# Tying the filler matmuls of layer 0's attention to the score product three key tiles back

## The chip, the cores and the metric

The kernel runs on one core of one Trainium2 chip. The metric is the device time of one execution in microseconds (us); lower is better. The core has five engines that work in parallel, each strictly through its own list of instructions: PE (TensorE, matrix products; its weight loads are shown as PEld), DVE (VectorE), ACT (ScalarE), POOL (GpSimd) and SP (SyncE, which issues the DMAs here). An instruction that needs another engine's result waits for a semaphore, and everything behind it on the same engine waits with it.

## What is computed

Two layers of a transformer over 1024 latent tokens and a prefix of 256 context tokens, width 1024, in 32-bit floats. Layer 0, which the change concerns, is attention in two head groups, each head with a SiLU gate:

```
aq, ak, av, ag, bq, bk, bv, bg = split_cols(h @ w_in, EVEN_WIDTHS)
oa = gqa_attend(qa_blk, ka, va)            # A: 8 heads, 2 KV heads, over all 1280 keys
ob = gqa_attend(qb, kk, vv, bias, sink)    # B: 8 heads, 2 KV heads, band of +-128 plus context, with a sink
y  = concat([oa * silu(ag), ob * silu(bg)]) @ w_out
x  = x + g * y
```

Here `h` is the RMS-normed input, scaled and shifted by vectors from `silu(c) @ mod_w + mod_b` ("modulation"). Layer 1 is a convolution module beside a neighbourhood attention, then a final norm.

## The kernel before

**Products in three parts.** To keep 32-bit precision each operand is split into a high and a low part (`split`, L298 a cast on ACT, L301 a subtraction on POOL or DVE), and `mm3` (L320 to L322) makes each product of high x high, high x low and low x high.

**Units and key tiles.** Layer 0's attention runs as four units, each one KV head with its four query heads, in the order `ORDER = (2, 3, 0, 1)`: units 2 and 3 are the window heads (B), units 0 and 1 the global heads (A). A unit has ten groups, one for each block of 128 queries; a group goes over 2 to 5 key tiles (B) or 2 or 10 (A). So there are 42 key tiles in a window unit and 84 in a global one, 252 in all.

**One group** (`attn_prep`, `attn_gen`). Ahead of a group its Q is loaded from DRAM (`QH`, `QL`), and the maximum of the scores is found: products `mx` (L578 for the context, L590 or L598 for the rest) into two PSUM banks, each reduced by DVE (L580, L591, L599), then `nmt` (L379 to L385), a transposition `trn` (L389), and L390, which writes the maximum into `QL`. For each key tile PE makes the score `st` in two halves, L467 with `QH` and L471 with `QL` (which holds the low part of Q and the maximum), into one of two PSUM banks; ACT takes the exponential (L479) and casts it (L298), POOL or DVE makes the low part (L301), and three tiles later (`LOOK0 = 3`) PE adds the three products with V into `ov` (L411 to L413), which has one bank. At the end of a group DVE divides (L421 to L424, L633, L635).

**Fill.** Between the steps of attention the kernel weaves other work, so that PE has something to do while attention waits for the other engines: the projections of the next unit (`proj_qkv`: products `pq`, with their transpositions `trk` in `qk_tail`), gate projections (`proj_gate`: `pg`), the modulation vectors (`mod_half_v`: multiply-adds `macc` of the DMAed `mw` on DVE, L221, and small sums `trm` on PE, L227), and in the last unit the output projection of the units already done (`out0`: `po`). `proj_qkv` writes K, Q and V to DRAM (L843, L844, L822) and they are loaded again (L553, L554, L565) when their unit is near. The buffers of K and V also serve for `mw` before the first unit.

**What sets the order.** `weave(main, nmain, fill, nfill, ...)` takes `nmain` steps of the attention generator (two steps for each key tile) and spreads `nfill` steps of fill over them. For the first three units it is called for a gate block, then for the next unit's projections (`NFILL` steps), then for the last `NLAST` steps, 28 in window units and 48 in global ones, with no fill. The written order is not the order on the chip: a scheduler goes over the program with a timeline of its own and picks, on each engine, the instruction of highest priority that is ready there. Fill is traced with a priority 80 places lower (`later(FL[0])`), so it comes in where the scheduler finds PE with nothing else, and it may then come in far ahead of its written place. `tc.issue_after(ins)` binds the instructions traced inside it, as far as they are on the engine of `ins`, to stand behind `ins` in that engine's list. It costs no semaphore and no instruction. `weave` has a parameter `lag` for this: with `lag = n` every fill step stands behind the score product L467 that is n back in `sts`, the list of all score products traced so far. Layer 1 uses it with 0, 0, 6 and 12; layer 0 leaves it at 0:

```python
                    if lag and len(sts) >= lag:
                        cx.enter_context(tc.issue_after(sts[-lag].ins))
                    next(fill, None)
```

Of the kernel before, what the change touches and what calls it, by code (L numbers as in the profile page):

```python
# [68 lines left out]
GB = 2  # L69
NFILL = (43, 43, 40)  # L70
GL = 12
HV = (('gggvvvvg',) * 3, ('gggvvvvg', 'vvvgvvvg', 'gggvvvvg'))
O1 = (6, 65, 41, 14)
TICK0, TICK1 = (1, 3)
# [15 lines left out]
def tile_kernel(ctx: ExitStack, tc: tile.TileContext, a, out):  # L90
# [406 lines left out]
    def weave(main, nmain, fill, nfill, last=True, all_fill=True, lag=0):  # L497

        done = 0
        for k in range(nmain):  # L500
            next(main, None)
            while done * nmain < (k + 1) * nfill:
                with ExitStack() as cx:
                    cx.enter_context(later(FL[layer[0]]))
# [3 lines that stand above are left out]
                done += 1  # L508
        if all_fill:
            for _ in fill:  # L510
                pass
        if last:
            for _ in main:
                pass
# [136 lines left out]
    NSTEP = (168, 84)  # L651


    with ExitStack() as p0x:
# [114 lines left out]
        def proj_gate(u, ms):  # L769

            if u not in gw:
                gw[u] = load_g0(u) if u == ORDER[0] else load_w0("ev_g", u, 256)
            wh, wl = gw[u]
            for m, c in ms:
                t0, n = CHUNKS[c]
                pp = bank("pp", nm("pg"))
                for dk in range(DK):
                    ms_ = slice(m * P, (m + 1) * P)
                    mm3(pp[:, :n], wh[dk][:, ms_], wl[dk][:, ms_], Hs(h, 0, t0, n, dk), Hs(h, 1, t0, n, dk),
                        dk == 0, dk == DK - 1)  # L780
                    if dk % 3 == 1:
                        tick()
                        yield
                sg = ap.tile([P, 640], F32, tag="rt2", name=nm("sg"), bufs=2)
                silu2(pp[:, :n], sg[:, :n])
                mark[0] = SY.dma_start(Gs[u][:, m, t0 : t0 + n], sg[:, :n])
                for _ in range(2):
                    if tails:
                        qk_tail(*tails.pop(0))
# [96 lines left out]
        for k in range(4):  # L886
            u = ORDER[k]
            n = NSTEP[u // 2] + (12 if k == 0 else 0)
            if k < 3:
                n0 = N0[1 + u // 2] if k else N0[0]  # L890
                n1 = n - n0 - NLAST[u // 2]
                weave(main, n0, proj_gate(u, gblocks(k)[1]), 9, False)
                weave(main, n1, fill0(k + 1), NFILL[k], False)
                weave(main, NLAST[u // 2], iter(()), 0, False)
            else:
                weave(main, GL, proj_gate(u, gblocks(k)[1]), 18 - 3 * GB, False)
        run(mods)


# [76 lines left out]
    with tc.tile_pool(name="o0", bufs=1, reuse_waits="tile", side="right") as op_:  # L976
        U1 = ORDER[-1]
# [88 lines left out]
                next(fp[0])  # L1066
                yield

        weave(main, O1[0], load_oh(parts[0]), 6, False)
        weave(main, O1[1], out0_part(parts[0]), 48, False)  # L1070
        weave(main, O1[2], chain(load_oh(parts[1]), out0_part(parts[1])), 30, False)
        ws = [load_w(op_, a["ev_wo"], e2 * 256, 256, 256, WO, lambda dk: "gv"[dk % 2], dks=final, rb=2) for e2 in range(4)]
        fp = [final_proj(c) for c in range(3)]
        nh = [norm_h(0, "st", "tr"), norm_h(1, "pp", "tr"), norm_h(2, "st", "tr")]
        weave(main, NSTEP[U1 // 2] - GL - O1[0] - O1[1] - O1[2], through_attention(), O1[3])
        a0x.close()
        solo[0] = True
        layer[0] = 1
# [564 lines left out]
```

## Time and profile before

| | |
|---|---|
| median of 3 runs | 1567.05 us |
| the three runs | 1563.86, 1573.72, 1567.05 us |
| span of the profiled execution (no other time of it is recorded) | 1569.6 us |
| mean granted TensorE clock | 0.961 |
| busy: PE, DVE, POOL, ACT | 1460.8, 1129.4, 830.0, 762.0 us |
| layer 0's attention, from its first score product to its last product with V | 160.6 to 911.9 us |

The page of the profile gives for each engine the busy time and its share of the span, and the chain of work that ended last, by engine. The windows view gives the same busy times for chosen stretches, with the TensorE clock that was granted in each (1.00 is full) and the share of the DMA engines. The timeline lists one engine's instructions by start time and length; products on PE are pipelined, so the distance of two starts tells the pace, not the length. In brackets stand an idle time before an instruction and what ended it. In names `x<-y,z`, x is written and y, z are read.

### The profile page before, as it was taken

Reading aid. Unit: us, or ns where it says so; the run is one execution under the profiler, and the core shown is the slowest. Engines: PE = TensorE matmul, PEld = TensorE weight load, DVE = VectorE, ACT = ScalarE, POOL = GpSimd, SP = SyncE. Lnnn points to the kernel's source line nnn. Section 1 sums busy time; section 2 is a strip of 40 time slices with the busy share of each in tenths; the row PEclk is TensorE's granted clock in tenths of the full one; section 3 lists DMA queues with packets and bytes.
Section 4 is the critical chain, followed back from the end, with each engine's and each line's share of the span. In section 5 each row is a group of like instructions: output and inputs, shape, how many; then the busy total and the mean of one; then the engine's idle time right before and its main releaser. Section 6 shows DMA issues by size and latency. Waiting matters only on the chain.

```text
span 1569.6 us, 22251 instructions
## 1 busy us (share of the span) xinstructions
PE 1460.8 (93%) x6984; PEld 1178.9 (75%) x6984; DVE 1129.4 (72%) x2172; ACT 762.0 (49%) x1545; POOL 830.0 (53%) x762
## 2 busy tenths in 40 slices
PE   6989999998999999899999889999999999899995
PEld 1878877876888677588887568888887787677784
DVE  4898896797768677455488668999654466776776
ACT  2721354545454754655555746443343445545472
POOL 1561463555465675756545756665443333444575
PEclk9899999999999999999999989999999999799897
DMA  9548245424431225612112022214547888889632
GB/s 337 190 142 260 87 142 167 132 67 125 154 116 47 67 91 167 224 47 61 48 38 85 14 94 61 81 58 148 177 154 224 237 229 242 248 231 251 187 95 108
DMA packets 199438, 221.03 MB, mean 141 GB/s; under 512 B 18956, under 2 KB 155352, under 8 KB 199320
## 3 DMA queue, kind: packets, MB, share of 16 engines
q1 hardware_dynamic: 192656, 208.04, 43.5%
q10 hardware_dynamic: 6664, 11.57, 2.3%
q8 instruction: 55, 0.90, 0.2%
q14 instruction: 63, 0.52, 0.1%
HBM read 159.51 MB, written 60.03 MB: 140 GB/s over the span
## 4 chain that ended last, share of the span: by engine, by line
PE 65%; DVE 14%; DMA 11%; issue 4%; POOL 2%; SPq 2%; ACT 1%; ACTq 0%; DVEq 0%; POOLq 0%
PE p L322 6%; PE p L321 6%; PE p L320 6%; PE ov L411 4%; PE ov L413 4%; PE ov L412 4%; PE po L320 4%; PE po L321 4%; PE po L322 4%; PE st L467 4%; PE st L471 4%; DMA mw<-in_mod_w_dram 3%; DVE macc L221 2%; PE pq L322 2%; PE pq L321 2%
## 5 line engine op out<-in xcount | busy, mean ns | idle before, releaser
L301 POOL TENSOR_TENSOR pl<-pf,ph 128x512 fp32r<-128x512 f32 (+4 forms) x321 | 393.7, 1237 | 320.1 <-ACT ph L298 260.0
L301 POOL TENSOR_TENSOR wl<-wr,wh 128x256 fp32r<-128x256 f32 (+2 forms) x256 | 197.5, 788 | 203.1 <-ACT wh L298 192.4
L479 ACT ACTIVATE pf<-st 128x512 f32<-128x512 f32 x284 | 167.3, 597 | 177.4 <-PE st L471 138.3
L298 ACT CAST ph<-pf 128x512 fp32r<-128x512 f32 (+4 forms) x364 | 210.5, 588 | 28.9 <-PE ov L412 21.5
L298 ACT CAST wh<-wr 128x256 fp32r<-128x256 f32 (+2 forms) x264 | 102.8, 404 | 172.9 <-DMA wr<-in_ev_qkv_dram 40.4
L320 PE MATMUL p<-hh,wh 128*128 128x512 f32 x448 | 177.5, 398 | 2.9 <-DVE spk L301 1.5
L321 PE MATMUL p<-hl,wh 128*128 128x512 f32 x448 | 178.0, 398 | 0.2 <-POOL hl L301 0.2
L322 PE MATMUL p<-hh,wl 128*128 128x512 f32 x448 | 175.9, 400 | 0.1
L467 PE MATMUL st<-QH,KAt 128*128 128x512 f32 (+4 forms) x364 | 145.4, 401 | 11.4 <-ACT pf L479 9.7
L411 PE MATMUL ov<-ph,Vt 128*128 128x512 f32 (+4 forms) x364 | 143.5, 394 | 9.7 <-ACT ph L298 5.0
L413 PE MATMUL ov<-pl,Vt 128*128 128x512 f32 (+4 forms) x364 | 144.1, 396 | 6.8 <-POOL pl L301 3.6
L471 PE MATMUL st<-QL,KBt 68*128 68x512 f32 (+4 forms) x364 | 139.0, 391 | 5.8 <-DVE QL L390 5.7
L412 PE MATMUL ov<-ph,Vt 128*64 128x512 f32 (+4 forms) x364 | 140.5, 386 | 0.0
L1122 DVE SCALAR_TENSOR_TENSOR cps<-U,taps,cps 128x512 f32<-128x512 f32 x184 | 124.3, 748 | 0.0
L591 DVE TENSOR_REDUCE mp<-mx 128x1 f32<-128x512 f32 x128 | 85.7, 682 | 42.5 <-PE mx L590 41.8
L221 DVE SCALAR_TENSOR_TENSOR macc<-mw,csil,macc 128x512 f32<-128x512 f32 x107 | 94.5, 901 | 17.5 <-DMA mw<-in_mod_w_dram 16.7
L320 PEld LDWEIGHTS p<-hh,wh 128*128 128x128 f32 x448 | 84.6, 189 | 23.6 <-DVE spk L301 1.7
L321 PEld LDWEIGHTS p<-hl,wh 128*128 128x128 f32 x448 | 84.5, 189 | 20.4 <-POOL hl L301 0.6
L322 PEld LDWEIGHTS p<-hh,wl 128*128 128x128 f32 x448 | 84.8, 189 | 20.1 <-POOL wl L301 0.6
L467 PEld LDWEIGHTS st<-QH,KAt 128*128 128x128 f32 x364 | 71.2, 196 | 33.4 <-ACT pf L479 17.6
L413 PEld LDWEIGHTS ov<-pl,Vt 128*128 128x128 f32 x364 | 71.1, 195 | 32.5 <-POOL pl L301 7.8
L411 PEld LDWEIGHTS ov<-ph,Vt 128*128 128x128 f32 x364 | 71.3, 196 | 27.3 <-ACT ph L298 8.4
(277 smaller groups left out, 3546.2 us busy)
## 6 DMA issues: line engine op xcount, KB each, us to landing
mw<-in_mod_w_dram SPq DMA_DIRECT2D x34, 512.0 KB, 5.9
Q<-qs SPq DMA_DIRECT2D x40, 256.0 KB, 2.7
QH<-Q SPq DMA_DIRECT2D x80, 128.0 KB, 2.8
wr<-in_od_d_dram SPq DMA_DIRECT2D x64, 128.0 KB, 2.7
mw<-in_mod_w_dram SPq DMA_DIRECT2D x28, 256.0 KB, 3.3
wr<-in_ev_qkv_dram SPq DMA_DIRECT2D x32, 192.0 KB, 3.6
KAt<-KD SPq DMA_DIRECT2D x16, 384.0 KB, 6.2
wr<-in_od_wo_dram SPq DMA_DIRECT2D x48, 128.0 KB, 3.2
```

Source lines behind the costliest of these rows:

```text
L221: VE.scalar_tensor_tensor(t, w, csil[:, dk, q : q + 1], t, op0=ALU.mult, op1=ALU.add)
L298: SC.copy(hi, src)
L301: (GP if leng == "g" else VE).tensor_tensor(lo, src, hi.bitcast(F32), op=ALU.subtract)
L320: PE.matmul(o, lh, rh, start=first, stop=False)
L321: PE.matmul(o, lh, rl, start=False, stop=False)
L322: done[0] = PE.matmul(o, ll, rh, start=False, stop=last)
L411: PE.matmul(o, V[:, 64:192], ph[:, :n], start=(t == 0), stop=False)
L412: PE.matmul(g.ov[0:64, q0 : q0 + n], V[:, 0:64], ph[:, :n], start=False, stop=False)
L413: pvs.append(PE.matmul(o, V[:, 64:192], pl[:, :n], start=False, stop=(last and g.sink is None)))
L467: sts.append(PE.matmul(st[:, :n], KA[:, cs], g.QH[:, q0 : q0 + n], start=True, stop=False))
L471: PE.matmul(st[:, :n], KB[0:68, cs], g.QL[0:68, q0 : q0 + n], start=False, stop=True)
L479: SC.activation(pf[:, :n], st[:, :n], AF.Exp, scale=1.0 if g.bias else SCALE)
```

## The change

All weave calls of layer 0 that have fill get `lag = 3`. So no PE instruction of a fill step may stand ahead of the first half (L467) of the score product that was third from last when the step was traced. While fewer than three score products are traced, there is no bound. Instructions of fill on DVE, ACT, POOL and SP are not bound by it, but they get their results from PE. All priorities, step counts and buffers stay.

```diff
+LAG0 = 3
...
-                weave(main, n0, proj_gate(u, gblocks(k)[1]), 9, False)
-                weave(main, n1, fill0(k + 1), NFILL[k], False)
+                weave(main, n0, proj_gate(u, gblocks(k)[1]), 9, False, True, LAG0)
+                weave(main, n1, fill0(k + 1), NFILL[k], False, True, LAG0)
                 weave(main, NLAST[u // 2], iter(()), 0, False)
             else:
-                weave(main, GL, proj_gate(u, gblocks(k)[1]), 18 - 3 * GB, False)
+                weave(main, GL, proj_gate(u, gblocks(k)[1]), 18 - 3 * GB, False, True, LAG0)
...
-        weave(main, O1[0], load_oh(parts[0]), 6, False)
-        weave(main, O1[1], out0_part(parts[0]), 48, False)
-        weave(main, O1[2], chain(load_oh(parts[1]), out0_part(parts[1])), 30, False)
+        weave(main, O1[0], load_oh(parts[0]), 6, False, True, LAG0)
+        weave(main, O1[1], out0_part(parts[0]), 48, False, True, LAG0)
+        weave(main, O1[2], chain(load_oh(parts[1]), out0_part(parts[1])), 30, False, True, LAG0)
...
-        weave(main, NSTEP[U1 // 2] - GL - O1[0] - O1[1] - O1[2], through_attention(), O1[3])
+        weave(main, NSTEP[U1 // 2] - GL - O1[0] - O1[1] - O1[2], through_attention(), O1[3], True, True, LAG0)
```

The order of the instructions shows what the scheduler makes of it. The line numbers of the changed kernel are one higher. First PE at the start of the attention, where the second halves of the first two scores stand; `pq_` and a number is one block of 24 projection products. Before, five whole blocks and most of a sixth (`pq_2039`) stand ahead of them:

```order
L320 MATMUL pq_2039<-wh_1460,hh_171 128x384
L321 MATMUL pq_2039<-wl_1461,hh_171 128x384
L322 MATMUL pq_2039<-wh_1460,hl_172 128x384
L320 MATMUL pq_2039<-wh_1466,hh_171 128x384
L321 MATMUL pq_2039<-wl_1467,hh_171 128x384
L471 MATMUL st_1527<-QL_1271,KBt_1254 128x512
L471 MATMUL st_1544<-QL_1271,KBt_1254 128x512
L322 MATMUL pq_2039<-wh_1466,hl_172 128x384
```

With the change, at the same two halves, the second block (`pq_1695`) follows them:

```order
L599 MATMUL mx_1484<-KAt_1262,QH_1282 128x384
L599 MATMUL mx_1487<-KAt_1262,QH_1282 128x384
L390 MATMUL trn_1391<-ident,nmt_1375 12x128
L579 MATMUL mx_1622<-KAt_1262,QH_1522 128x256 x2
L579 MATMUL mx_1639<-KAt_1262,QH_1522 128x256 x2
L472 MATMUL st_1527<-QL_1271,KBt_1254 128x512
L472 MATMUL st_1544<-QL_1271,KBt_1254 128x512
L599 MATMUL mx_1643<-KAt_1262,QH_1522 128x384
L599 MATMUL mx_1675<-KAt_1262,QH_1522 128x384
L468 MATMUL st_1585<-QH_1270,KAt_1262 128x512
L472 MATMUL st_1585<-QL_1271,KBt_1254 128x512
L321 MATMUL pq_1695<-wh_1430,hh_169 128x384
```

Only one block is left ahead of these halves; the maximum products of the second and third group have moved up between the first maximum and its score.

The second place is PE near the end of the first unit (key tile 28, `st_2735`), whose maximum comes through `QL_2418`. Before, the next unit's projections stand in the gaps:

```order
L320 MATMUL pq_3280<-wh_3275,hc_168 128x384
L321 MATMUL pq_3339<-wl_3270,hc_168 128x384
L322 MATMUL pq_3339<-wh_3269,hc_168 128x384
L320 MATMUL pq_3339<-wh_3275,hc_168 128x384
L321 MATMUL pq_3280<-wl_3276,hc_168 128x384
L322 MATMUL pq_3280<-wh_3275,hc_168 128x384
L321 MATMUL pq_3339<-wl_3276,hc_168 128x384
L322 MATMUL pq_3339<-wh_3275,hc_168 128x384
L598 MATMUL mx_2878<-KAt_1262,QH_2730 128x256
L471 MATMUL st_2735<-QL_2418,KBt_1254 128x512
```

With the change the same score stands among attention alone:

```order
L414 MATMUL ov_2782<-pl_2704,Vt_1255 128x512
L417 MATMUL ov_2782<-QL_2168,sk 128x512
L599 MATMUL mx_2856<-KAt_1262,QH_2730 128x256
L599 MATMUL mx_2869<-KAt_1262,QH_2730 128x256
L390 MATMUL trn_2688<-ident,nmt_2678 12x128
L599 MATMUL mx_2875<-KAt_1262,QH_2730 128x256
L599 MATMUL mx_2878<-KAt_1262,QH_2730 128x256
L472 MATMUL st_2735<-QL_2418,KBt_1254 128x512
```

The `pq` products have moved behind, into the next unit's written place.

The third place is PE near the end of the last unit (key tile 240, `st_9476`). Before, the output projection is already done there:

```order
L411 MATMUL ov_9389<-ph_9419,Vt_1259 128x512
L412 MATMUL ov_9389<-ph_9419,Vt_1259 64x512
L467 MATMUL st_9476<-QH_8876,KAt_5695 128x512
L471 MATMUL st_9476<-QL_8877,KBt_1258 128x512
L413 MATMUL ov_9389<-pl_9420,Vt_1259 128x512
L411 MATMUL ov_9389<-ph_9444,Vt_1259 128x512
L412 MATMUL ov_9389<-ph_9444,Vt_1259 64x512
```

With the change its blocks `po` stand between the key tiles:

```order
L321 MATMUL po_9368<-hh_7480,wh_9227 128x512
L322 MATMUL po_9368<-hl_7481,wh_9227 128x512
L323 MATMUL po_9368<-hh_7480,wl_9228 128x512
L468 MATMUL st_9476<-QH_8876,KAt_5695 128x512
L472 MATMUL st_9476<-QL_8877,KBt_1258 128x512
L412 MATMUL ov_9389<-ph_9444,Vt_1259 128x512
L413 MATMUL ov_9389<-ph_9444,Vt_1259 64x512
L321 MATMUL po_9402<-hh_7480,wh_9233 128x512
```

So fill has moved from the middle of the unit to its end. From layer 1 on PE's order is the same in both.

## The prediction

> **What bounds the kernel now.** I read the page's busy times first, then the chain of work that ended last, then the windows view over stretches cut at the score products of layer 0, then the waits of PE inside the poor stretches.
>
> ```profile
> PE 1460.8 (93%) x6984; PEld 1178.9 (75%) x6984; DVE 1129.4 (72%) x2172; ACT 762.0 (49%) x1545; POOL 830.0 (53%) x762
> ...
> PE 65%; DVE 14%; DMA 11%; issue 4%; POOL 2%; SPq 2%; ACT 1%; ACTq 0%; DVEq 0%; POOLq 0%
> ```
>
> PE is busy for 93% of the span and makes 65% of the chain. So time moves only if PE idles less, or runs at a lower granted clock for a shorter time. Layer 0's attention has 252 key tiles (window heads 0 to 83, global heads 84 to 251); I count them by their first score product (L467) in the order of PE. The next rows are the windows view, cut where the tiles 0, 6, 12, 24, 48, 54, 60, 72, 90, 114, 120, 126, 144, 156, 228 and 246 start; the first row is the time just before tile 0 and the last the tail. Columns: length, busy time by engine, granted PE clock, DMA.
>
> ```profile
> 152.30:160.60 8.30, 7.88 (x53) 7.66 (x53) 7.05 (x12) 1.26 (x3) 2.18 (x3) 1.00 0.77 234
> 160.60:191.30 30.70, 30.24 (x172) 27.88 (x171) 25.94 (x57) 10.87 (x25) 14.94 (x12) 1.00 0.22 66
> 191.30:206.60 15.30, 12.68 (x51) 8.46 (x51) 14.32 (x29) 7.44 (x18) 7.82 (x7) 0.78 0.20 61
> 206.60:248.50 41.90, 39.56 (x207) 32.23 (x206) 37.08 (x77) 23.10 (x57) 29.16 (x26) 1.00 0.53 162
> 248.50:347.30 98.80, 96.22 (x502) 82.80 (x500) 77.48 (x170) 44.33 (x94) 48.45 (x39) 1.00 0.40 123
> 347.30:359.90 12.60, 10.78 (x51) 7.64 (x51) 10.72 (x27) 7.88 (x19) 6.20 (x5) 1.00 0.19 54
> 359.90:387.10 27.20, 21.36 (x113) 17.84 (x111) 21.58 (x56) 11.98 (x28) 13.70 (x13) 0.99 0.45 139
> 387.10:445.30 58.20, 56.88 (x284) 47.16 (x284) 45.48 (x96) 27.27 (x61) 28.10 (x25) 0.95 0.50 155
> 445.30:503.30 58.00, 58.00 (x300) 51.89 (x299) 42.32 (x80) 28.01 (x54) 33.98 (x28) 1.00 0.23 68
> 503.30:543.30 40.00, 36.72 (x156) 25.08 (x155) 25.48 (x49) 28.00 (x47) 28.69 (x23) 1.00 0.15 42
> 543.30:560.80 17.50, 16.71 (x90) 14.76 (x89) 13.13 (x24) 10.68 (x23) 12.87 (x12) 1.00 0.39 119
> 560.80:576.60 15.80, 12.92 (x48) 9.27 (x47) 10.49 (x20) 8.08 (x17) 11.75 (x11) 0.78 0.20 60
> 576.60:638.90 62.30, 59.94 (x294) 47.32 (x293) 47.24 (x77) 35.75 (x64) 38.76 (x26) 1.00 0.57 177
> 638.90:665.40 26.50, 22.41 (x89) 16.56 (x88) 9.40 (x18) 15.41 (x29) 21.25 (x21) 0.87 0.67 221
> 665.40:852.90 187.50, 187.50 (x892) 151.56 (x892) 117.69 (x211) 99.02 (x181) 106.13 (x91) 1.00 0.18 52
> 852.90:891.50 38.60, 34.77 (x140) 23.84 (x138) 26.68 (x46) 24.21 (x44) 24.02 (x20) 0.91 0.13 45
> 891.50:914.00 22.50, 15.56 (x61) 10.77 (x62) 18.02 (x27) 14.70 (x26) 13.67 (x10) 0.81 0.03 9
> ```
>
> I call "loss" the length less PE's busy time, plus the missing share of the clock times the length. From the second row on: 0.5, 6.0, 2.3, 2.6, 1.8, 6.1, 4.2, 0, 3.3, 0.8, 6.4, 2.4, 7.5, 0, 7.3 us: 51.2 us in 731 us, of which 42.4 after tile 24. This is all that any reordering here can win. It sits where fill is missing. Counting the fill matmuls of each stretch in the order of before, and giving each 0.175 us (384 wide) or 0.23 us (512 wide), from the spacing of rows quoted below, the rows at 191.30, 347.30, 503.30, 560.80, 638.90 and 852.90 hold 0.4, 0.4, 0.3, 0.3, 3.5 and 3.2 us of fill for 72 tiles, and lose 32.3 us. The row at 665.40 holds 90 us of fill for 72 tiles and loses nothing.
>
> Loss per tile from these rows, the prices of everything below:
> - window heads without fill: (6.0 + 1.8) / 12 = 0.65 us, ends 0.30 and 1.0;
> - window heads with fill: 2.6 + 6.1 + 4.2 over the 54 tiles from 24 on that have it (72 to 83 lose nothing): 0.24 us;
> - global heads without fill: (3.3 + 6.4 + 7.5 + 7.3) / 60 = 0.41 us, ends 0.14 (row 503.30) and, over more than one group, 0.63 (row 638.90);
> - global heads with fill: (0.8 + 2.4) / 102 = 0.03 us.
>
> **The change, part by part.** It adds no instruction and no semaphore; only the place of PE rows moves, and what other engines then get later. The fill's own PE work is the same in both. Three terms follow.
>
> *The start, tiles 0 to 24.* These rows of PE's timeline show the first maximum products (L578), the first halves of the first two scores, two neighbours of the 384-wide fill, and the second halves (L471, which need the maximum in QL).
>
> ```profile
> 160.06 0.70 PE L578 MATMUL mx<-KAt,QH 128*128 128x256 f32 x4 [0.42 <-DMA V<-vs]
> 160.59 0.63 PE L467 MATMUL st<-QH,KAt 128*128 128x512 f32 x2
> ...
> 161.58 0.34 PE L321 MATMUL pq<-wl,hh 128*128 128x384 f32 x1
> 161.76 0.34 PE L322 MATMUL pq<-wh,hl 128*128 128x384 f32 x1
> ...
> 182.13 0.62 PE L471 MATMUL st<-QL,KBt 68*128 68x512 f32 x2
> ```
>
> Before, 31 fill matmuls fill the time up to 160.06, and 109 more stand between there and the second half of the score at 182.13, so the chain from maximum to QL costs PE next to nothing. Now 7 of the 31 and all of the 109 stand behind it: 24 are ahead of L471 instead of 140. At 152.30 PE finds only two mod reductions and then waits for KAt, whose load SP issued here:
>
> ```profile
> 157.16 1.28 SPq L553 DMA_DIRECT2D KAt<-K  x3
> ```
>
> That load follows the last reading of its buffer by a mod product on DVE, and in the new DVE order two more mod instructions stand ahead of that one: about 1.2 us later, so the first maximum product starts near 161.3. From there DVE sets the pace: PE may go ahead only as DVE hands back the two mx banks. Between the first maximum and QL the new DVE order has 4 L580, 8 L599 (four of 256, four of 384, each with its readout), 7 mod products and one L390.
>
> ```profile
> L221 DVE SCALAR_TENSOR_TENSOR macc<-mw,csil,macc 128x512 f32<-128x512 f32 x30 | 27.9, 939 | 6.8 <-DMA mw<-in_mod_w_dram 6.4
> L580 DVE TENSOR_REDUCE mp<-mx 128x2 f32<-128x512 f32 x16 | 10.7, 683 | 0.9 <-PE mx L578 0.9
> L599 DVE CUSTOM_DVE_ANT_0 mx<-mx,k_bm 128x384 f32<-128x384 f32 x18 | 10.0, 563 | 2.1 <-PE mx L598 1.9
> L390 DVE TENSOR_TENSOR QL<-trn,k_bd 12x512 fp32r<-12x512 f32 x6 | 4.1, 682 | 0.2
> L599 DVE DVE_READ_ACCUMULATOR2_ANT mp<- 128x1 f32 x22 | 2.8, 126 | 0.1
> L599 DVE CUSTOM_DVE_ANT_0 mx<-mx,k_bm 128x256 f32<-128x256 f32 x4 | 1.7, 420 | 0.0
> ```
>
> 4 x 0.683 + 4 x 0.420 + 4 x 0.563 + 8 x 0.126 + 7 x 0.939 + 0.682 = 14.9 us, on from about 161.7: QL near 176.6, against 182.13. Attention starts 5.5 us earlier, but with 116 x 0.175 = 20.3 us less fill done, so PE is 14.8 us behind. What comes back: at tile 24 both orders have done the same fill (138 to 139 us by the count). Before needed 66.4 us from 182.1 to 248.5, of which 8.8 were loss, so 57.6 of work. Now it is 57.6 + 20.3, less 1.5 for the maximum products already done, = 76.4: tile 24 at 253.0 with no loss at all, at 257.6 with 0.19 us per tile (row 206.60: 2.3 over 12 filled tiles). That is +4.5 to +9.1 us. I take +9.1, since rows with fill in the window heads do lose. It cannot be much under +4.5, PE's own floor. DVE, busy for 14.32 of 15.30 us in row 191.30 and 37.08 of 41.90 in row 206.60, has the same work to do up to tile 24 and is no further behind, so it adds no term of its own.
>
> *The ends of units.* The order now keeps to the written plan, with no fill in the last steps of each unit. Tiles 30 to 36 and 72 to 84, which held 7.5 and 13 us of fill, now hold 0 and 2; tiles 144 to 162 held 12 and hold none; 126 to 144, 162 to 168 and 180 to 192 hold 16 us where 55 stood. At these places the second half of a score waits for QL with only attention in between. Such a wait is in the trace:
>
> ```profile
> 385.88 0.73 PE L471 MATMUL st<-QL,KBt 68*128 68x512 f32 x2 [4.47 <-DVE QL L390]
> ```
>
> Prices: 18 window tiles without fill x 0.65 = 11.7 (ends 5.4 and 18). 18 global tiles without fill x 0.41 = 7.4; 36 with a little fill at half of that, 7.4 (together ends 5 and, with no credit and at 0.63, 34).
>
> *The places that get fill.* Tiles 48 to 54, 90 to 114 with 120 to 126, and 228 to 246, whose rows held 0.3 to 3.2 us, now get 14, 34 and 21 us, mostly 6 to 7 us for six tiles, which is what the row at 665.40 has (90 us for 72). They are priced as filled. The other 42 window tiles from 24 on: 42 x 0.24 = 10.1. The other 108 global tiles: 108 x 0.03 = 3.2. The tail behind tile 246 (row 891.50) has the same order of PE but for one sum of squares, and costs nothing new: the 13 last blocks of out-projection stand between it and the first product that needs its result.
>
> After tile 24: 11.7 + 7.4 + 7.4 + 10.1 + 3.2 = 39.8 against 42.4, so -2.6 us. The sum is +9.1 - 2.6 = +6.5 us on the profiled 1569.6, 1576.1; that execution lies 2.55 us over the median of the three runs, so 1573.5 against 1567.05. SP and POOL: the loads of Q for the next groups now stand ahead of a V write that waits for fill, which only helps; the splits of weights on ACT and POOL are not bound and stay hidden behind PE.
>
> **A rule of the clock.** These rows show PE's products before and after the longest gap between 191.3 and 206.6, 1.44 us: 512-wide products follow each other at 0.43 us after it and at 0.24 again from 202.48 on, and the clock of row 191.30 is 0.78.
>
> ```profile
> 197.78 0.79 PE L467 MATMUL st<-QH,KAt 128*128 128x512 f32 x1 [1.44 <-ACT pf L479]
> 200.50 0.63 PE L412 MATMUL ov<-ph,Vt 128*64 128x512 f32 x1
> 200.93 0.63 PE L413 MATMUL ov<-pl,Vt 128*128 128x512 f32 x1
> 202.48 0.40 PE L411 MATMUL ov<-ph,Vt 128*128 128x512 f32 x1
> 202.72 0.40 PE L412 MATMUL ov<-ph,Vt 128*64 128x512 f32 x1
> ```
>
> [...] I keep the rows' prices; as a rival this lies within 1%, and I give it 0.05.
>
> **Rivals.**
> 1. *Slower: the QL wait of each group.* In the poor stretches nothing covers the chain from maximum to QL, so each group of heads waits there. 18 window tiles are about 4 groups, 54 global ones about 5: 9 waits at the 4.47 us of row 385.88 are 40 us against the 26.5 priced above, so +13.7: 1587. It passes 1% (1582.7) when a wait is over about 4.1 us. For it: row 385.88, and the 6.0 us of row 191.30. Against it: row 503.30 loses 3.3 us over two and a half groups without fill.
> 2. *Faster: even fill is worth more than its price.* If filled window tiles lose nothing, as 445.30 shows, global ones without fill 0.14, and the start +4.5: 11.7 + 2.5 + 2.5 + 3.2 = 19.9, so -22.5 + 4.5 = -18.0: 1549. Against it: rows 359.90 and 387.10 have fill and still lose 10.3 us.
> 3. *No effect: the poor stretches only change places.* The start stays at PE's floor, +4.5, the rest is -2.6: 1569. That the edit does nothing at all is excluded by the order, in which most PE rows of layer 0's attention move.
>
> **How the numbers follow.** A measurement of this kernel can tell about 1%, 15.7 us, from no change: 1551.4 to 1582.7. My forecast, rival 3 and the clock's case lie within it, together 0.60; rival 1 has 0.28, rival 2 has 0.12. The predicted time is the sum, 1573. Ends: all cheap ends together give +4.5 + (5.4 + 5 + 10.1 + 3.2 - 42.4) = -14.2, about 1553; the dear ones +9.1 + (18 + 34 + 10.1 + 3.2 - 42.4) = +32, 1599. With rival 2 a little under the cheap end and rival 1 at 1587, I give 1551 to 1594 for 8 in 10.
>
> **What would show it.** Right: PE idle between 153 and 177 of about 15 us, the first L471 near 177, tile 24 later than 248.5 by 4 to 9 us; windows at tiles 90 to 126 and 228 to 246 with PE full and the clock at 1.00; new losses of about 0.65 us a tile at 30 to 36 and 72 to 84 and 0.4 at 144 to 162. Wrong: no loss at the unit ends (then it is faster), waits of more than 4 us for QL at each group (slower), or a moved loss in layer 1, whose order is the same.

## The result and the profile after

The changed kernel took 1604.74 us (median of 4 runs, 1603.14 to 1609.25), the kernel before 1570.38 us beside it (4 runs, 1563.86 to 1575.45): ratio 1.0247, 95% interval 1.0211 to 1.0283. It is slower by 2.5%. The prediction was 1573 us with a range of 1551 to 1594; the measured time lies above it.

The busy times of the page of the changed kernel (span 1603.9 against 1569.6):

```profile
PE 1476.2 (92%) x6984; PEld 1185.4 (74%) x6984; DVE 1132.6 (71%) x2172; ACT 762.2 (48%) x1545; POOL 831.6 (52%) x762
```

PE is busy 15 us longer for the same 6984 products, and the rest of the 34 us is idle time. The windows view of the changed kernel, cut at tiles 0, 6, 12, 24, 30, 36, 42, 72, 84, 126, 144, 162, 168, 180, 192, 228 and 246, and the row behind tile 246 (columns as in the prediction):

```profile
161.30:192.20 30.90, 26.89 (x116) 22.17 (x116) 20.46 (x55) 10.24 (x25) 10.40 (x9) 0.79 0.16 49
192.20:212.20 20.00, 19.65 (x110) 17.57 (x108) 15.91 (x29) 7.63 (x17) 11.61 (x10) 1.00 0.18 53
212.20:261.00 48.80, 44.91 (x234) 38.18 (x232) 41.15 (x77) 24.53 (x58) 31.73 (x27) 0.97 0.49 148
261.00:291.90 30.90, 24.22 (x112) 17.36 (x110) 22.95 (x67) 10.41 (x25) 5.11 (x4) 0.92 0.50 158
291.90:304.30 12.40, 11.73 (x37) 8.52 (x38) 4.97 (x8) 8.51 (x17) 8.43 (x7) 0.64 0.15 44
304.30:321.60 17.30, 15.47 (x81) 12.53 (x80) 12.39 (x36) 8.60 (x17) 7.00 (x6) 1.00 0.22 69
321.60:448.00 126.40, 120.86 (x619) 102.48 (x617) 99.13 (x216) 57.65 (x131) 72.31 (x57) 1.00 0.43 133
448.00:475.40 27.40, 25.23 (x108) 18.81 (x109) 22.24 (x47) 16.95 (x32) 15.52 (x12) 0.88 0.24 73
475.40:591.70 116.30, 115.28 (x572) 97.74 (x571) 81.57 (x144) 61.26 (x115) 70.51 (x56) 1.00 0.23 70
591.70:642.20 50.50, 43.63 (x203) 31.93 (x202) 39.73 (x71) 28.60 (x57) 34.60 (x31) 0.93 0.44 133
642.20:672.20 30.00, 27.63 (x110) 17.71 (x109) 17.32 (x32) 22.19 (x38) 22.23 (x18) 1.00 0.13 38
672.20:687.20 15.00, 13.84 (x57) 9.68 (x56) 7.92 (x17) 8.32 (x15) 9.17 (x8) 1.00 0.03 10
687.20:723.40 36.20, 36.20 (x161) 28.70 (x161) 13.53 (x25) 19.33 (x31) 21.19 (x14) 1.00 0.39 125
723.40:751.40 28.00, 22.53 (x82) 16.10 (x81) 11.46 (x20) 18.08 (x33) 22.84 (x17) 0.82 0.76 261
751.40:876.80 125.40, 125.17 (x605) 101.41 (x605) 76.67 (x138) 53.27 (x104) 60.42 (x57) 1.00 0.16 49
876.80:920.70 43.90, 43.82 (x204) 34.90 (x202) 32.67 (x53) 24.99 (x47) 24.75 (x20) 1.00 0.10 37
...
920.70:1603.90 683.20, 627.84 (x2950) 508.01 (x2950) 483.97 (x946) 323.73 (x672) 344.94 (x362) 0.96 0.55 164
```

Read by the prediction's measure (length less PE busy, plus the missing clock), the losses down the rows are 10.5, 0.4, 5.4, 9.2, 5.1, 1.8, 5.5, 5.5, 1.0, 10.4, 2.4, 1.2, 0, 10.5, 0.2, 0.1: 69.2 us where there were 51.2. The rows that were poor before, 84 to 126 and 228 to 246, are full now. The start loses 10.5 us in tiles 0 to 6, where the kernel before lost 6.0 one row later. Behind it three rows stand out: 24 to 30 (9.2), 126 to 144 (10.4) and 180 to 192 (10.5). The same three stretches before, from its windows view (the second stands in the prediction):

```profile
248.50:297.00 48.50, 47.02 (x253) 40.52 (x252) 33.37 (x79) 19.45 (x42) 17.09 (x16) 1.00 0.62 189
...
731.20:762.70 31.50, 31.50 (x155) 25.70 (x154) 15.78 (x33) 16.50 (x31) 17.19 (x15) 1.00 0.12 34
```

They lost 1.5, 2.4 and 0, with 34, 31 and 17 us of fill, counted and priced as in the prediction; now they have 8, 9 and 4.

Where the 34.3 us lie: tile 24 comes 12.5 us later (261.0 against 248.5), the way from tile 24 to tile 246 is 16.7 us longer (659.7 against 643.0, the same fill in both), and the part behind tile 246 is 5.1 us longer (683.2 against 678.1).

PE's waits from tile 24 into the tail, changed kernel (engine, line, tile, releaser: us in total, times, longest):

```profile
PE mx L591 <- DVE mp L592: 6.2, 9, 1.8
PE ov L412 <- ACT ph L299: 4.3, 3, 2.6
PE ov L414 <- DVE pl L302: 3.5, 2, 2.4
PE st L468 <- ACT pf L480: 3.1, 6, 1.2
...
PE trn L390 <- DVE modT L229: 2.6, 1, 2.6
...
PE bc L264 <- DVE nr L244: 2.3, 1, 2.3
```

No wait is long. The largest sum is that of the maximum products for a bank that DVE has not read yet. The second half of a score waits for QL less than before; the same view from tile 24 to tile 246, kernel before and changed kernel:

```profile
PE st L471 <- DVE QL L390: 5.7, 2, 4.5
...
PE st L472 <- DVE QL L391: 1.2, 3, 0.7
```

### The profile page after: what moved, and what is told of

It reads as the page before. It is cut to its first block, busy times and chain, and to the rows that moved or that the text cites. A ratio compares the mean times of both kernels' runs of the same rounds, so it can differ in the third digit from the quotient of the medians.

```text
span 1603.9 us, 22241 instructions
## 1 busy us (share of the span) xinstructions
PE 1476.2 (92%) x6984; PEld 1185.4 (74%) x6984; DVE 1132.6 (71%) x2172; ACT 762.2 (48%) x1545; POOL 831.6 (52%) x762
## 5 line engine op out<-in xcount | busy, mean ns | idle before, releaser
L412 PE MATMUL ov<-ph,Vt 128*128 128x512 f32 (+4 forms) x364 | 143.4, 394 | 10.4 <-ACT ph L299 7.1
L472 PE MATMUL st<-QL,KBt 68*128 68x512 f32 (+4 forms) x364 | 141.4, 396 | 3.2 <-DVE QL L391 3.2
```

The lines of the kernel that those rows point to most:

```text
L412: PE.matmul(o, V[:, 64:192], ph[:, :n], start=(t == 0), stop=False)
L472: PE.matmul(st[:, :n], KB[0:68, cs], g.QL[0:68, q0 : q0 + n], start=False, stop=True)
```

## The experiments

Two theories stood after the result. "Places": each stretch pays by itself for the fill that it lacks. "Late start": the late first maximum leaves other work behind, and the later stalls follow from it. The times of the kernel before are those taken beside each group of runs: 1564.85, 1565.48, 1567.16, 1567.11 and 1567.48 us. The experiments carry the numbering of the kernel before, so their lines are one less than those of the changed kernel. The edits are shown shortened, as what differs from the changed kernel. The nine numbers of LAG0 belong to the weaves in the order of the code: gates and fill of unit 1, gates and fill of units 2 and 3, gates of unit 4, and the four weaves of the out-projection; a single number stands for all nine. The loss of a stretch always comes from one profiled execution.

**The parts of the change: units and weaves**

The lag on the first unit's weaves alone:

```diff
-LAG0 = 3
+LAG0 = (3, 3, 0, 0, 0, 0, 0, 0, 0)
```

> The bound only on the fill woven into the first unit (key tiles 0 to 42). In the order of instructions the fill then stands as in the changed kernel up to tile 24 and as in the kernel before from tile 48 on. Theory 'places' (each stretch of attention pays by itself for the fill that it lacks): the changed kernel reached tile 24 12.5 us later than before, and nothing behind it changes, so +9 to +13 us, about 1581. Rival 'late start' (the late start leaves the modulation products and K, Q loads behind, and the later stalls follow from that): most of the 34 us, +25 to +34, about 1600.

Measured: 1574.55 us, ratio 1.0077 (1.0047 to 1.0108).

The lag on the middle units' weaves alone:

```diff
-LAG0 = 3
+LAG0 = (0, 0, 3, 3, 3, 0, 0, 0, 0)
```

> The bound only on the fill woven into the second and third unit and on the last gate block; the start is as before. From tile 30 on the fill stands as in the changed kernel. Theory 'places': the profiles of before and after differ by +15 us of loss between tiles 24 and 42, -8 to 72, +7 to 84, -11 to 126, +10 to 168, +11 to 192, -8 to 246 and +5 in the tail: together about +21 us, 1591. Rival 'late start': without the late start these stalls are not there, 0 to +8 us.

Measured: 1588.87 us, ratio 1.0161 (1.0126 to 1.0195). The losses of 13.5 us at 24 to 30, 9.5 at 126 to 144 and 13.5 at 174 to 192 are there without a late start.

The lag on the out-projection's weaves alone:

```diff
-LAG0 = 3
+LAG0 = (0, 0, 0, 0, 0, 3, 3, 3, 3)
```

> The bound only on the output projection woven into the last unit. Fill stands as before up to tile 144, then none until tile 174, then as in the changed kernel from tile 204 on. Theory 'places': 30 tiles without fill at the 0.32 us a tile that tiles 144 to 162 lost after the change cost 10 us, the stop at tiles 180 to 192 some more, up to 10; tiles 144 to 156 and 228 to 246 cost before 7.7 and 10.1 us, of which the latter goes; the tail +5: in all +3 to +12, about 1578. Rival 'late start': 0, as nothing at the start changes.

Measured: 1569.58 us, ratio 1.0021 (0.9998 to 1.0044). The three ratios multiply to 1.0261, the whole change's 1.0247 within its interval. The first two runs decide against the late start: the parts pay where they lie, about 12 us for the first unit and 25 for the middle. The out-projection costs 3 us or nothing, which does not separate the two theories.

**A longer lag**

```diff
-LAG0 = 3
+LAG0 = 12
```

> All fill bound as in the change, but behind the score product 12 key tiles back instead of 3. The start is then as before; fill is 5 to 16 us further ahead than in the changed kernel at tiles 36 to 108 and as late as there at 130 to 144. Theory 'places': about half of the loss outside the start, +8 to +16 us, about 1582. Rival 'late start': 0 to +4, as the start is that of before.

Measured: 1597.55 us, ratio 1.0207 (1.0171 to 1.0243). Both theories missed: they had expected at most 16 us over the kernel before, and it is 32.7. The losses at 24 to 30, 126 to 144 and 174 to 192 are 13.4, 13.1 and 8.5 us: twelve tiles of lead are not enough to fill them, and the gain at 42 to 72 and 84 to 126 is mostly gone. So three is not an unlucky number: a bound four times as far back costs nearly as much.

**What makes a thin stretch dear: the modulation, or missing cover**

Layer 1's modulation sums left out as far as they fall into layer 0's attention, in the changed kernel and in the kernel before:

```diff
         for dk in range(DK):
+            if l and not solo[0] and not pre:
+                yield
+                continue
...
         for n_, (q, t) in enumerate(zip(conds, accs)):
+            if l and not solo[0]:
+                continue
```

> The changed kernel with layer 1's modulation sums left out as far as they lie in layer 0's attention (the products macc on VectorE, their loads, their trm products; layer 1's modulation is then partly constants, so the output differs). It stands beside the same omission in the kernel before. Theory 'side work': a stretch with thin fill is dear because what comes with the fill on other engines (modulation sums, their loads, and the trm products that stand in PE's row waiting for them) still runs there, so without the sums the loss in tiles 24 to 30 falls from 11.5 to about 4 us and in 126 to 144 from 14.1 to about 7, and the time stands only about 20 us over its partner instead of 34. Rival 'cover': PE rows are simply missing there, so 24 to 30 loses 10 us or more again and the time stands 30 us or more over its partner.

> The kernel before with the same modulation sums left out. Both theories: a few us under the kernel before, for the trm products on PE are about 2.4 us of work and the stretch 42 to 72, which loses 18 us, is where VectorE is busiest; 1555 to 1565 us. It is the partner of the run above and tells nothing by itself.

Measured: 1585.09 us (ratio 1.0114, 1.0091 to 1.0137) and 1548.68 us (0.989, 0.9865 to 0.9915): the changed one stands 36.4 us over its partner. The windows view of the first, tiles 24 to 30 and 126 to 144:

```profile
253.30:278.00 24.70, 22.48 (x92) 16.37 (x91) 16.21 (x47) 9.38 (x23) 5.10 (x4) 0.86 0.45 139
...
569.40:619.60 50.20, 42.88 (x206) 31.63 (x205) 40.30 (x72) 29.00 (x57) 32.29 (x29) 0.97 0.45 137
```

They still lose 5.7 and 8.8 us, and the partner 0 and 2.5. So the modulation takes 3.5 us of the first (9.2 in the changed kernel) and 1.6 of the second (10.4), and is not the main cause. Neither theory's numbers came for the stretches; the 36.4 us over the partner are the rival's (30 or more).

But a lack of cover alone does not price these rows either: 144 to 162 has no fill at all and lost 2.4 us for 18 tiles, 126 to 144 has 9 us of fill and lost 10.4. The groups of DVE's instructions in the changed kernel, tiles 126 to 144 (first fence) and 144 to 162 (second):

```profile
L592 DVE TENSOR_REDUCE mp<-mx 128x1 f32<-128x512 f32 x19 | 12.5, 682 | 0.3
L581 DVE TENSOR_REDUCE mp<-mx 128x2 f32<-128x512 f32 x6 | 3.9, 684 | 3.4 <-PE mx L579 3.4
L302 DVE TENSOR_TENSOR qs<-trk,qs 128x384 fp32r<-128x384 f32 x7 | 3.8, 549 | 2.5 <-ACT qs L299 2.4
L636 DVE SCALAR_TENSOR_TENSOR y<-y,gt 128x256 f32<-128x256 f32 x3 | 2.9, 960 | 0.0
```

```profile
L592 DVE TENSOR_REDUCE mp<-mx 128x1 f32<-128x512 f32 x14 | 9.3, 682 | 0.4 <-PE mx L591 0.4
L581 DVE TENSOR_REDUCE mp<-mx 128x2 f32<-128x512 f32 x4 | 2.6, 688 | 9.1 <-PE mx L579 9.1
```

For the same 18 tiles the first stretch has 25 readings of maxima against 18, beside the last splits of Q and K (qs). DVE is busy for 39.7 of 50.5 us there and for 17.3 of 30.0 in the other; 4.5 of these 22.4 us more are maxima, the rest is the projections' and other work. The extra maxima come from a short group: two groups of each unit (query blocks 0 and 1) have two key tiles only, and while such a group runs, the maxima of its neighbours are prepared close together. Query block 1 stands seventh in a unit, at tiles 26 and 27 in the first unit and 136 and 137 in the third.

**Moving the short groups**

Query block 1 next to last, in all units but the last, with the lag of the change:

```diff
-QORD = (2, 3, 4, 0, 5, 6, 1, 7, 8, 9)
+QORD = (2, 3, 4, 0, 5, 6, 7, 8, 1, 9)
```

> The changed kernel with the groups of each unit but the last in another order: the second short group (query block 1, two key tiles) comes eighth-last place later, next to last, in place of seventh. The fill by tile stays within 2 us of the changed kernel's everywhere. Theory 'short groups': thinly filled stretches are dear where a short group brings the maximum products of three groups close together (tiles 24 to 30 and 126 to 144), and VectorE reads them beside the projections' last work; then the loss in 126 to 144 falls from 10.4 to about 5 us and in 24 to 30 from 9.2 to about 5, and comes back at 30 to 42 and 144 to 162 (there 7.0 and 2.4 now). Rival 'projection ends': VectorE's own work for the projections (splits and rotations of Q and K) makes them dear wherever the short group stands: 126 to 144 keeps 9 us or more, 24 to 30 8 us or more. For the whole time both allow 1595 to 1610.

Measured: 1588.00 us, ratio 1.0155 (1.0118 to 1.0192). Tiles 24 to 30 and 126 to 144 in its windows view:

```profile
263.00:286.90 23.90, 21.24 (x96) 16.63 (x96) 15.63 (x43) 10.80 (x25) 5.54 (x5) 0.90 0.61 185
...
589.50:630.10 40.60, 38.21 (x189) 30.11 (x188) 29.90 (x54) 28.11 (x57) 32.38 (x29) 0.92 0.41 124
```

They lose 5.0 and 5.6 us, as the theory of the short groups expected, and the loss does not come back at 30 to 42 (3.3) or 144 to 162 (3.0); 42 to 72 pays 13.0 instead of 5.5. The time is under the range that both theories had allowed; of the 18.6 us between this execution and the changed kernel's, 7.1 lie behind tile 246.

Both short groups early, with the lag and without:

```diff
-QORD = (2, 3, 4, 0, 5, 6, 1, 7, 8, 9)
+QORD = (2, 0, 3, 1, 4, 5, 6, 7, 8, 9)
```

> The changed kernel with both short groups early in every unit (query blocks in the order 2, 0, 3, 1, 4 to 9), where the held-back fill still flows. Fill by tile within 7 us of the changed kernel's everywhere. Theory 'short groups': 126 to 144 falls from 10.4 to about 5 us, 24 to 30 from 9.2 to about 5, the filled stretches at 84 to 126 and 42 to 72 pay at most 3 us more: 1592 to 1600. Rival 'projection ends': losses stay, 1600 to 1610.

> The kernel before (no lag) with both short groups early in every unit. Tells whether the order of the groups is worth something by itself, and so how much of the run above belongs to the lag. Theory 'short groups': the loss of 7.3 us at 228 to 246 and of 10.0 at 84 to 126 changes place; 84 to 126 with no fill pays 5 us more, 228 to 246 about 5 less: within 1% of the kernel before. Rival: the same.

Measured: 1598.92 us (ratio 1.0206, 1.0166 to 1.0245) with the lag, 1577.24 us (1.0074, 1.0042 to 1.0106) without. With it, 126 to 144 loses 5.1 us as expected; 24 to 30 keeps 8.6, the rival's number, and 42 to 72 pays 14.5 instead of 5.5, which neither expected. But in this order VectorE still reads 13 maxima in tiles 24 to 30, against 14 in the changed kernel and 6 in the late order, so this stretch is no test of the theory. Without the lag the time stays within the 1% that was expected. In this order the lag costs 21.7 us.

The late order (query block 1 next to last) without the lag:

```diff
-LAG0 = 3
+LAG0 = 0
```

> The kernel before (no lag) with the second short group next to last in every unit but the last. Theory 'place': the lag was dear because it took the cover from the short groups; with them moved the lag costs less, so without lag this order brings little: 1560 to 1570, and the lag's price in this order is 18 to 28 us instead of 34. Rival 'lag alone': the lag costs 34 us in any order, and this order is worth 16 us by itself: about 1553, faster than before by 0.8 to 1.2%.

Measured: 1566.91 us, ratio 1.0003 (0.9985 to 1.0022). In this order the lag costs 1588.00 - 1566.91 = 21.1 us, in the old order 34. So the late order is worth nothing without the lag and takes about 13 us off the price of the lag, as the theory of the place had expected. By the windows, 6.3 of the 13 lie where the short groups stood: the lag adds 7.7 and 8.0 us of loss at 24 to 30 and 126 to 144 in the old order, 4.6 and 4.8 in the late one. The rest lies elsewhere, 4.1 of it in tiles 12 to 24, where the late order loses 6.4 us without the lag and the old one 2.3. The place of the short groups is shown for about 6 of the 34 us; the rest of the 13 is not explained.

The late order with the lag only in the middle and at the last pieces, and then with the fourth unit's gates free too, which leaves layer 1's rows on PE as in the kernel before:

```diff
-LAG0 = 3
+LAG0 = (0, 0, 3, 3, 3, 0, 0, 0, 3)
...
+LAG0 = (0, 0, 3, 3, 0, 0, 0, 0, 3)
```

> The same order of groups with the lag only from the second unit on up to the fourth unit's gates, and at the last pieces; the first unit's fill and the first out-projection pieces run ahead. Theory 'place': the start's 12 us are saved against the full lag in this order (1588), and the loss in 24 to 30 is about 5, in 126 to 144 about 5.6, in 174 to 192 about 8: 1570 to 1578. Rival 'lag alone': the middle units cost what they cost in the old order (+25 over the run above).

> The second short group next to last in every unit but the last, the lag only on the fill of units 2 and 3 (tiles 24 to 138) and on the last pieces, and layer 1's rows on TensorE in the order of the kernel before. Theory 'place': the thin stretch at 24 to 30 pays about 8 us, the even fill at 84 to 126 returns about 9, the last pieces 2 to 7: 1558 to 1570, no slower than the kernel before. Rival 'lag alone': it keeps most of the +25 us that the lag of the middle units cost in the old order: 1580 or more.

Measured: 1590.28 us (ratio 1.0143, 1.0124 to 1.0162) and 1580.38 us (1.0077, 1.0051 to 1.0102). Both lie above what the theory of the place expected and at the rival's numbers (1566.91 and 25 more; 1580 or more). Where the time lies tells more than the total. The windows view behind tile 246 of the first, and of the late order without lag:

```profile
895.60:1588.00 692.40, 630.70 (x2950) 509.92 (x2950) 480.37 (x946) 323.59 (x672) 347.09 (x362) 0.95 0.54 162
```

```profile
893.20:1564.20 671.00, 623.39 (x2942) 504.29 (x2942) 477.40 (x943) 323.50 (x670) 343.89 (x359) 0.96 0.55 165
```

Of the 23.8 us between these two executions 21.4 lie behind tile 246, where layer 1's rows on PE stand in another order (by the names of the rows in the traces, some 180 and 300 of the last 2600 differ from the kernel before). From tile 24 to tile 246 the first of these kernels, in which the last pieces are bound as well, is 8.2 us longer than the late order without lag (642.3 against 634.1); in the old order the lag on the middle units had made this part 21.4 us longer (664.4 against 643.0). So the rival's reason does not hold, though its number came. In the second run, whose last 2600 PE rows are those of the kernel before, tile 246 comes at 899.8, 6.6 us later than in the late order without lag.

Tiles 24 to 30 lose 9.7 and 9.9 us in these two. Compared at the same lag, moving the short group lowers this stretch by about 4 us both times (9.2 to 5.0 with the lag everywhere, 13.5 to 9.7 with it on the middle units) and 126 to 144 by about 5 (10.4 to 5.6, 9.5 to 4.3). What is left at 24 to 30 is larger where less fill stands there: counted in the traces, 2.1 and 2.2 us in these two kernels and 6.5 in the late order with the lag everywhere. That a lag in layer 0 can change the order of layer 1 was not foreseen by me; in the changed kernel itself those rows are the same as before.

**Tiles 180 to 192: GpSimd's splits, or the issues on ScalarE**

```diff
-OCE, ODE, OHE = ('v', 'g', 'g')
+OCE, ODE, OHE = ('v', 'g', 'v')
```

> The changed kernel, but the subtraction that splits the attention's output for the out-projection runs on VectorE instead of GpSimd. Theory 'side work': in tiles 174 to 192 GpSimd is bound by three 128x1024 splits of 2.4 to 2.8 us each and hands pl and the weights' low halves over late, so the loss there falls from 11.0 to about 4 us and the time from 1604 to about 1598. Rival 'cover': the loss there stays at 9 us or more and the time within 3 us of the changed kernel's.

Measured: 1608.31 us, ratio 1.0266 (1.0244 to 1.0287). The loss of 174 to 192 falls from 10.7 to 7.3 us, but 10 us of fill moved into the stretch, and the time did not fall. The run does not show GpSimd's splits as the bound.

In the changed kernel, ScalarE's rows just before PE's longest wait there, and PE's row:

```profile
734.82 4.09 ACTq L1000 DMA_DIRECT2D x<-in_xT_dram  x2
739.01 0.62 ACT L299 CAST ph<-pf 128x512 fp32r<-128x512 f32 x1 [3.62 <-DMA gt<-G]
```

```profile
739.68 0.49 PE L412 MATMUL ov<-ph,Vt 128*128 128x512 f32 x1 [2.58 <-ACT ph L299]
```

Two DMA issues take 4.09 us on ScalarE's queue. One exponential of 0.60 us runs beside their start, then ScalarE idles for 3.62 us; the cast starts when the issues end (739.01 and 738.91), and PE waits 2.58 us for it. (The bracket puts the end of the idle time down to the landing of a gate, `gt`.) The 12 loads moved to SyncE:

```diff
-            SC.dma_start(x1[c][:, es], ...)
+            SY.dma_start(x1[c][:, es], ...)
```

> The changed kernel with the 12 loads of the residual (x) issued by SyncE instead of ScalarE. In the changed kernel two of these issues take 4.09 us on ScalarE's queue while the DMA engines are 93% busy, and the cast to ph behind them is late, for which TensorE waits 2.58 us. Theory 'issue': the loss in tiles 174 to 192 falls from 10.7 to 5 to 7 us, the time by 3 to 6 us to about 1600. Rival 'full DMA': the loads of weights and x are late whoever issues them, the loss stays within 2 us of 10.7.

Measured: 1599.26 us, ratio 1.0218 (1.0186 to 1.0249). Tiles 180 to 192:

```profile
727.60:751.10 23.50, 19.89 (x76) 13.90 (x75) 11.31 (x20) 18.24 (x32) 22.07 (x16) 0.85 0.89 306
```

The loss of these tiles falls from 10.5 to 7.1 us, the upper end of what the theory of the issue expected, and on SyncE's queue no row of these issues takes over 1.63 us; the total is 5.5 us lower, but its interval overlaps that of the changed kernel. The DMA engines are busy for 89% of the stretch, 76% in the changed kernel.

Another run bears the issues out. With the splits on VectorE the same 12 issues stand on ScalarE's queue, but no row of them takes over 0.90 us, and tiles 174 to 192 lose 7.3 us, where 10 us of fill had moved in as well. With the loads on SyncE they lose 7.0, in the changed kernel, with its row of 4.09 us, 10.7. So about 3 us of the 10.7 go with the issues.

The other 7 us go with the gates of the fourth unit. The two kernels of the late order with the lag in the middle differ only in whether these gates are bound; their tiles 174 to 192, bound first:

```profile
680.80:726.30 45.50, 41.72 (x170) 30.07 (x169) 16.94 (x31) 28.69 (x49) 37.34 (x26) 0.92 0.65 217
...
724.40:770.50 46.10, 46.10 (x230) 37.71 (x229) 26.08 (x48) 23.22 (x44) 26.17 (x24) 1.00 0.15 43
```

They lose 7.4 and 0.0 us, with 13.5 and 22.7 us of fill counted in the traces. In the run with the lag on the out-projection's weaves alone, where the gates are free as well, these tiles lose 0.4. So the bound on the gates makes them dear. The amount of fill alone does not settle it: with the splits on VectorE 23.4 us of fill stood there, and 7.3 us were lost. Freeing the gates does not bring tile 246 forward, though (899.8 against 895.6): 144 to 162 loses 6.6 instead of 3.6, and other stretches more too.

**The last pieces alone: a version that might beat the kernel before**

The lag on the last weave alone, with the old order of groups (3 tiles) and with the late one (6 tiles):

```diff
-LAG0 = 3
+LAG0 = (0, 0, 0, 0, 0, 0, 0, 0, 3)
...
+LAG0 = (0, 0, 0, 0, 0, 0, 0, 0, 6)
```

> Only the last of the eight weaves (the out-projection's last pieces, tiles 222 to 246) is held back by three key tiles, all others run ahead as before. By the prices of the stretches: tiles 228 to 246 get about 13 us of fill and lose about 2 us instead of 10, tiles 222 to 228 lose their fill and pay about 2 us: 5 to 8 us under the kernel before, ratio 0.995 to 0.997. Rival, that holding fill back is bad wherever it is done (the fill's results come later): 0 to +5 us over the kernel before.

> The same order of groups, the lag only on the last weave (six key tiles), layer 1's rows on TensorE in the order of the kernel before. By the prices of the stretches 228 to 246 gets 10 us of fill instead of 4.6 and loses 2 us less; with layer 1 unchanged 1555 to 1565, at best 0.7% under the kernel before. Rival: no gain, 1565 to 1570.

Measured: 1569.72 us (ratio 1.0027, 1.0011 to 1.0043) and 1573.47 us (1.0027, 1.0004 to 1.0050). The windows view of the first, tiles 222 to 228 and 228 to 246:

```profile
833.90:845.00 11.10, 8.55 (x33) 5.05 (x32) 10.81 (x22) 5.84 (x12) 7.27 (x6) 1.00 0.17 49
845.00:883.20 38.20, 38.16 (x178) 29.90 (x177) 25.69 (x45) 26.36 (x48) 26.90 (x21) 1.00 0.22 73
```

The stretches behave as priced (7.3 us saved at the end, 2.6 paid ahead of it), and tile 246 comes at 883.2 instead of 891.5 in this one execution; the times of 12 runs of each show no gain. The first lies where the rival had it, the second above what either had allowed. Where the gain goes is not settled: by the names of the rows in the traces, layer 1's order differs from the kernel before in some 170 rows in the first kernel, and in hardly any in the second. No version that was tried beats the kernel before.

## Why the prediction was wrong

- **What bounds the kernel**: right. PE's idle and slow-clock time moved most, +18.0 of the 34.3 us in the rows above.
- **The start, +9.1**: right in kind, too small. The first L471 (L472 now) begins at 176.97, where 176.6 was worked out:

```profile
156.19 1.84 PE L228 MATMUL trm<-one,macc 128*128 128x2 f32 x8 [3.41 <-DVE macc L222]
160.27 1.20 PE L579 MATMUL mx<-KAt,QH 128*128 128x256 f32 x4 [2.25 <-issue]
...
173.06 1.22 PE L599 MATMUL mx<-KAt,QH 128*128 128x384 f32 x2 [1.94 <-DVE mp L581]
...
176.97 1.19 PE L472 MATMUL st<-QL,KBt 68*128 68x512 f32 x2
```

  From there to tile 24 it is 84.0 us, 7.6 over the work of 76.4, where 4.6 was taken. So 12.5 instead of 9.1. That 176.97 and 176.6 agree is in part luck: the first maximum product came at 160.27, not near 161.3, and DVE, taken as busy all the way, idled 2.5 us before the first QL. Between 153 and 177 PE idled 9.4 us where about 15 was foretold, at a clock of 0.66.
- **18 window tiles without fill, 11.7**: right; 30 to 36 and 72 to 84 lost 5.1 + 5.5 = 10.6.
- **18 global tiles without fill, 7.4**: 2.4 measured.
- **36 global tiles with a little fill "at half of that, 7.4"**: the step that failed. 126 to 144, 162 to 168 and 180 to 192 lost 10.4 + 1.2 + 10.5 = 22.1, more than the 14.8 that the prediction's own price (0.41 a tile) gives for no fill at all. The price was taken per tile and by the amount of fill, between "none" and "full". The runs showed that what else stands there counts more: at 126 to 144 about half of the loss goes when the short group moves away (10.4 to 5.6), and at 174 to 192 about 3 of 10.7 us go with the DMA issues on ScalarE and the other 7 when the fourth unit's gates are not bound.
- **The other 42 window tiles, "priced as filled", 10.1**: 16.5 measured, of which 9.2 in the six tiles 24 to 30, priced 1.4. They had 8 us of fill instead of 34, and were counted as filled because they had some.
- **The places that get fill, 3.2 for 108 tiles**: right; 1.3 measured.
- **The tail, "costs nothing new"**: neither shown nor refuted. It took 5.1 us longer in this execution, and 2.27 of it is PE's wait for the norm of a chunk (bc, L264, for nr), which is not there in the kernel before. But the late order with the lag has this wait too (2.3), and its tail took 676.1 us, less than the 678.1 before; kernels with the same order of layer 1 took 676 to 688.
- In sum after tile 24: 52.9 where 39.8 was added up and 42.2 stood before. That is 10.7 of the 16.7 us. The other 6.0 are PE time that the loss does not count, products that take longer than the mean clock of their stretch explains; no term of the prediction covers them, and why they are there is open.
- **Rival 1**, the wait for QL of each group, gave the right sign, but not by its mechanism: it asked for 40 us in nine waits of 4.47 us, and from tile 24 to 246 PE waits for QL three times, 1.2 us in all. **Rival 2** had 4.5 us for the start and 19.9 us of loss behind tile 24; 12.5 and 52.9 came. **Rival 3** had the start at +4.5 and the rest at -2.6; 12.5 and 21.8 came.
- **The clock**: the granted clock's share of the loss went from 16.8 to 26.8 us (missing share times length, summed over the rows). The row 291.90:304.30 has a clock of 0.64; the longest gap in the 17 us ahead of its start is this one, and there is none over 1 us in it:

```profile
287.75 0.38 PE L390 MATMUL trn<-ident,nmt 128*12 128x128 f32 x1 [2.65 <-DVE modT L229]
289.27 0.98 PE L599 MATMUL mx<-KAt,QH 128*128 128x256 f32 x2 [1.14 <-DVE mp L600]
```

  512-wide products follow each other at 0.43 us in this row up to 300.36 and at 0.23 to 0.25 from 300.78 on. So a clock of 0.64 stands behind a longest gap of 2.65 us here, and one of 0.78 beside a longest gap of 1.44 us in the prediction's row. The clock's case (the poor stretches lose no clock), to which the prediction gives 0.05 and which is no term of its sum, is shown by no run: the clock's share of the loss was 16.8 us before and 26.8 after. Keeping the rows' own prices, which hold the lost clock, was right.

Open: what is left of the loss at 24 to 30 and 126 to 144 once the short group is moved, half of the 13 us that the late order saves under the lag, the 6.0 us of slower products, and why the gain at the last pieces does not reach the end.

## What to carry to other kernels

Fill that runs ahead of its plan need not be waste: here it lay where other engines' chains needed cover (tiles 24 to 30 lost 1.5 us with 34 us of fill and 9.2 with 8). Before a lag or an even spread is put on it, price each stretch by what the attention does there (how many maxima or other short chains stand close together, and what the fill still runs on other engines), not by an average per tile. A stretch with a little fill can be dearer than one with none: here 126 to 144 lost 10.4 us with 9 us of fill, and 144 to 162, of as many tiles, 2.4 with none.

## What the runs showed of the hardware

- A clock of 0.64 over 12.4 us behind gaps of 2.65 and 1.14 us, and of 0.79 over 30.9 us behind gaps of 3.41 and 2.25 us, with two more of 1.18 and 1.94 us in it.
- Two DMA issues on ScalarE's queue took 4.09 us in a stretch where the DMA engines were busy for 76% (row 723.40:751.40, 261 GB/s), and ScalarE did nothing beside them but one exponential of 0.60 us; the rows of the other ten issues of the same loads took 0.34 to 0.98 us. The longest row of these loads took 1.34 us in the kernel before and 0.90 us with the splits on VectorE, both on ScalarE's queue, and 1.63 us on SyncE's.
- The part behind tile 246 took 671 to 692 us over these kernels, and 676 to 688 us in the seven whose last 2600 rows on PE are the same: single executions differ there by several us.
